# Two phases with buffers of their own for the expert stages of a one-core network

## The chip, the cores and the metric

The kernel runs on one core of a Trainium2 chip. What counts is the device time of one execution, in microseconds. Three executions of the kernel before took 4761.98, 4771.15 and 4781.52 us (median 4771.15).

## The reference

The reference runs two networks one after the other. The first has two layers (`DEPTH` 2); each has a token mixer and then an expert stage, `peer_ffn`, for 256 context tokens and 256 latent tokens of width 1024 (in layer 1 for the latent tokens alone). The second has four layers of attention-like mixers and feed-forward stages. The change touches the two expert stages only:

```python
def peer_ffn(h, wq, subkeys, u, v):
    qr = (h @ wq).astype(jnp.float32).reshape(bsz, t, PEER_HEADS, 2, PEER_HALF)
    scores = jnp.einsum('bthpd,hpkd->bthpk', qr, subkeys.astype(jnp.float32))
    s1, i1 = lax.top_k(scores[..., 0, :], PEER_TOPK)
    s2, i2 = lax.top_k(scores[..., 1, :], PEER_TOPK)
    ...
    top, pos = lax.top_k(cand, PEER_TOPK)
    eidx = jnp.take_along_axis(cidx, pos, axis=-1)
    gate = jax.nn.softmax(top, axis=-1).astype(h.dtype)
    ...
        act = jax.nn.gelu(jnp.einsum('ted,td->te', u[ek], hk), approximate=False)
        return jnp.einsum('te,ted->td', gk * act, v[ek])
```

Each token chooses 16 experts in each of 8 heads out of 16,384 (128 x 128 keys). An expert is a row of `u` and a row of `v`: Gelu of the product with the row of `u`, times the gate, weighs the row of `v`.

## The kernel before

`peer(l)` runs the expert stage of layer l. The first F tokens (128 of 512 in layer 0, 64 of 256 in layer 1) are "fetched": `fetched` gathers the chosen rows of `u` and `v` by indirect DMAs on the POOL queue, 1 MB each, and works on VectorE (two 1024-wide steps a gather). The other ND tokens (384 and 192) are "dense": they are multiplied with all experts, and the gates, zero for experts not chosen, pick them out. The experts come in 128 steps j of 128 experts.

*Routing.* `route` is a generator. `c_q` makes queries and scores, `choose` the top 16 of pairs, `gates` the softmax, and `spread` writes the gates as a dense matrix: for four tokens at a time one-hot rows of i1 (`oa`) and of i2 times the gate (`ob`) on VectorE, four small matmuls, two copies out of PSUM on ScalarE, and then a store to the DRAM tensor G in blocks of 32 tokens.

*First product.* `u_act` multiplies step j of `u` with the dense tokens. In layer 0 the weight and the tokens are split into a high and a low part (`load_w`, `split`: a copy on ScalarE, a subtraction on VectorE), and each of the 8 k-chunks takes three matmuls: high by high, high by low, low by high. In layer 1 (`whole`) the f32 weight is used as it is loaded. `ahead` makes first products during the routing and stores the sums to the DRAM tensor U. How many, and between which routing steps, is set by the costs that `route` yields: as long as PE's sum `tp` is below VectorE's sum `td`, another first product is put in. Layer 0 makes all 128 in the routing. In layer 1, 72 are made there, and the rest in the second phase.

*Second product.* `u_phase(j0)` prepares two steps: loads of the gates G (four steps a load, in runs of 4 x 32 x 4 = 512 bytes) and of the sums U, Gelu, the product with the gate, and the split into high and low, `wt`. For steps that were not made early it calls `u_act`. `v_phase` loads the rows of `v`, splits them and multiplies. In layer 0 the dense tokens are the stationary side: 18 matmuls of 512 columns a step, into six PSUM banks. In layer 1 `v` is: 24 matmuls of 192 columns a step into four banks, two chunks to a bank. The loops are written so that `u_phase` of one pair of steps stands ahead of `v_phase` of the pair before. Beside this, `extra` computes modulation vectors (layer 0) and gathers that are left go on.

*Order and buffers.* All loads and stores here but the gathers are issued by SP in one order. A scheduler orders the instructions by priority (mostly program order) and readiness; each tag has so many buffers, and an instruction that writes a buffer waits for its last reader. Weights of `u` and of `v` share the tag `wraw` (4 buffers in layer 0, 6 in layer 1); `whi` and `wlo` are their high and low parts. `part` opens pools of buffers for the routing (`ROUTE`) and, when these are closed, for the second product (`DENSE`), in the same memory.

Of the kernel before, what the change touches and what calls it, by code (L numbers as in the profile page):

```python
# [10 lines left out]
F32 = mybir.dt.float32  # L11
# [11 lines left out]
P = 128  # L23
# [28 lines left out]
WORKP = (dict(nbig=2048, bufs=4, ga=3, w=(4, 3, 2), mm=2, sm=6, sp=4, uv=4, H=1, acc=1),  # L52
         dict(nbig=2048, bufs=2, ga=3, w=(6, 2, 2), mm=4, sm=4, sp=6, uv=5, H=1, acc=1, xw=1))
ROUTE = dict(bufs=3, rt=1, VI=1, t=3, r=13, alt=1, oa=2, ob=4)
DENSE = dict(bufs=1, gt=2, ad=2, wt=2, o=2)
# [28 lines left out]
class Kern:  # L84
# [634 lines left out]
    def route(self, l, xh, xl, cs, G, F, fetch):  # L719
# [93 lines left out]
        def spread(t):  # L813
            for t0 in range(*own(t), GT):
                st = [self.b8().rearrange("p (j t) -> p j t", t=GT) for _ in range(2)]
                for t4 in range(t0, t0 + GT, 4):
                    pg = self.ps()
                    a = self.t(512, tag="oa").rearrange("p (t n) -> p t n", t=4)
                    nc.vector.tensor_tensor(a, self.iotaf[:, None, :].to_broadcast([P, 4, P]),
                                            i1T[:, t4:t4 + 4, None].to_broadcast([P, 4, P]), op=OP.is_equal)  # L820
                    for i in range(4):
                        t_ = slice(t4 + i, t4 + i + 1)
                        b_ = self.t(P, tag="ob")
                        nc.vector.tensor_scalar(b_, self.iotaf, i2T[:, t_], gT[:, t_], op0=OP.is_equal, op1=OP.mult)
                        nc.tensor.matmul(pg[:, i * P:(i + 1) * P], a[:, i], b_, start=True, stop=True)
# [57 lines left out]
    def peer(self, l, extra=()):  # L883
# [8 lines left out]
        xh, xl = self.big(KD, N, F32R), self.big(KD, N, F32R)  # L892
# [35 lines left out]
        self.part(routing, **ROUTE)  # L928
# [40 lines left out]
        while early < late:  # L969
            ahead()  # L970
            early += 1
# [1020 lines left out]
```

## Time and profile before

| | |
|---|---|
| median of three runs | 4771.15 us |
| profiled execution | 4776.65 us |
| its span, first to last instruction | 4774.9 us |
| mean granted TensorE clock | 0.953 |
| PE busy | 4352.2 us (91%) |
| VectorE (DVE) busy | 3402.8 us (71%) |
| ScalarE (ACT) busy | 2104.5 us (44%) |
| moved by DMA | 948.85 MB, mean 199 GB/s |

A busy PE is a matmul in flight; matmuls overlap, so the duration of one is longer than the distance between two. The clock is given as a share of 2.4 GHz; its other level is 1.2 GHz. The DMA share is the mean busy share of the core's 16 DMA engines. Line numbers (L949) are those of the kernel before, and a tile's name stands for all its buffers. L208 is every activation, L275 and L280 are the subtractions that make a low part, L293 is a matmul of `linear`. L949 and L944 are first products (layer 0 and 1), L1026 and L1019 second products (layer 0 and 1), L825 the small matmuls of `spread`.

### The profile page before, as it was taken

How to read it: one execution, taken by the hardware profiler on the slowest of the kernel's cores; microseconds unless marked ns; L12 is line 12 of the kernel's file. 1: busy time of each engine (PE TensorE's matmuls, PEld its weight loads, DVE VectorE, ACT ScalarE, POOL GpSimd, SP SyncE). 2: the span in 40 equal slices, each digit the busy share in tenths (PEclk: the TensorE clock that was granted, in tenths of full speed). 3: DMA queues.
4: the chain of work that ended last, by engine and by line, in shares of the span. 5: the costliest groups of instructions: out<-in, count | busy, mean ns of one | idle time of the engine just before them, and what ended most of it. 6: DMA issues, size and time to landing. Idle time of an engine off the chain costs nothing. (4 is left out here: it accounts for less than half of the span.)

```text
span 4774.9 us, 72861 instructions
## 1 busy us (share of the span) xinstructions
PE 4352.2 (91%) x27964; PEld 3992.4 (84%) x27964; DVE 3402.8 (71%) x6651; ACT 2104.5 (44%) x4022; POOL 288.9 (6%) x200
## 2 busy tenths in 40 slices
PE   6999798998988999998967799989999999999999
PEld 5887798888876787887856699978998998899799
DVE  9987998899778757978863344477567567566765
ACT  4443344344433445541323233377445454445853
POOL 0000022222011100001220000000000000000000
PEclk8999899999999999999977799999999998999999
DMA  5413388888999874547994468533553553055255
GB/s 191 133 58 104 136 291 323 295 309 329 327 305 337 281 223 130 169 160 282 377 376 146 148 204 266 193 99 103 175 152 108 175 159 100 19 172 165 90 168 172
DMA packets 313101, 948.85 MB, mean 199 GB/s; under 512 B 28832, under 2 KB 130080, under 8 KB 282928
## 3 DMA queue, kind: packets, MB, share of 16 engines
q1 hardware_dynamic: 285104, 742.86, 47.4%
q0 software_dynamic: 27648, 201.34, 11.2%
q8 instruction: 219, 3.59, 0.3%
q14 instruction: 130, 1.06, 0.1%
HBM read 872.70 MB, written 71.04 MB: 198 GB/s over the span
## 5 line engine op out<-in xcount | busy, mean ns | idle before, releaser
L208 ACT ACTIVATE whi<-wraw 128x1024 fp32r<-128x1024 f32 (+1 forms) x924 | 964.3, 1047 | 1337.0 <-PE MM L293 524.3
L293 PE MATMUL MM<-xhl,whi 128*128 128x272 f32 (+1 forms) x4736 | 934.6, 293 | 6.7 <-ACT whi L208 6.1
L275 DVE TENSOR_TENSOR wlo<-wraw,whi 128x1024 fp32r<-128x1024 f32 (+2 forms) x668 | 799.3, 1198 | 161.2 <-PE MM L293 53.1
L293 PE MATMUL MM<-b,whi 128*128 128x272 f32 (+2 forms) x3712 | 855.3, 323 | 59.8 <-ACT b L208 50.0
L293 PEld LDWEIGHTS MM<-xhl,whi 128*128 128x128 f32 x4736 | 751.2, 190 | 27.4 <-issue 10.0
L293 PEld LDWEIGHTS MM<-b,whi 128*128 128x128 f32 x3712 | 623.0, 192 | 115.8 <-ACT b L208 56.5
L293 PE MATMUL MM<-xhl,wlo 128*128 128x272 f32 (+1 forms) x2368 | 689.2, 291 | 2.8 <-DVE wlo L275 2.7
L293 PE MATMUL MM<-b,wlo 128*128 128x272 f32 (+2 forms) x1856 | 597.2, 323 | 5.3 <-DVE wlo L275 4.7
L949 PE MATMUL MM<-b,whi 128*128 128x384 f32 x2048 | 545.4, 347 | 14.2 <-ACT ga L208 13.9
L280 DVE TENSOR_TENSOR wlo<-wraw,whi 128x1024 fp32r<-128x1024 f32 x256 | 311.3, 1222 | 277.4 <-ACT whi L208 206.4
L1019 PE MATMUL SM<-wt,whi 128*128 128x192 f32 x2048 | 399.0, 300 | 103.2 <-ACT whi L208 76.1
L293 PEld LDWEIGHTS MM<-xhl,wlo 128*128 128x128 f32 x2368 | 448.7, 190 | 10.2 <-DVE wlo L275 4.6
L873 POOL DMA_INDIRECT uv<-uv,sp x192 | 287.9, 1499 | 2676.1 <-DVE acc L869 952.0
L1019 PEld LDWEIGHTS SM<-wt,whi 128*128 128x128 f32 x2048 | 352.6, 215 | 106.9 <-ACT whi L208 79.3
L949 PE MATMUL MM<-b,wlo 128*128 128x384 f32 x1024 | 356.0, 349 | 59.0 <-DVE wlo L275 59.0
L949 PEld LDWEIGHTS MM<-b,whi 128*128 128x128 f32 x2048 | 380.2, 195 | 18.6 <-ACT ga L208 17.9
L1026 PE MATMUL SM<-whi,wt 128*128 128x512 f32 x1536 | 380.7, 397 | 13.7 <-ACT wt L208 8.0
L293 PEld LDWEIGHTS MM<-b,wlo 128*128 128x128 f32 x1856 | 355.7, 192 | 31.2 <-DVE wlo L275 10.0
L944 PE MATMUL MM<-xw,wraw 128*128 128x192 f32 x2048 | 359.1, 332 | 10.5 <-ACT ga L208 9.9
L1026 PEld LDWEIGHTS SM<-whi,wt 128*128 128x128 f32 x1536 | 293.7, 192 | 82.1 <-ACT wt L208 10.7
L944 PEld LDWEIGHTS MM<-xw,wraw 128*128 128x128 f32 x2048 | 339.7, 194 | 12.5 <-ACT ga L208 11.6
L1019 PE MATMUL SM<-wt,wlo 128*128 128x192 f32 x1024 | 305.0, 298 | 15.2 <-DVE wlo L280 15.2
(488 smaller groups left out, 6096.8 us busy)
## 6 DMA issues: line engine op xcount, KB each, us to landing
wraw<-uT SPq DMA_DIRECT2D x256, 512.0 KB
wraw<-uv SPq DMA_DIRECT2D x256, 512.0 KB
wraw<-w_gate_up SPq DMA_DIRECT2D x176, 512.0 KB
g<-b SPq DMA_DIRECT2D x36, 1024.0 KB
wraw<-w_in SPq DMA_DIRECT2D x64, 512.0 KB
wraw<-fox_w_in SPq DMA_DIRECT2D x64, 512.0 KB
wraw<-w_down SPq DMA_DIRECT2D x64, 512.0 KB
wmod<-wmodT SPq DMA_DIRECT2D x56, 512.0 KB
```

The source lines that it names most:

```text
L208: r = nc.scalar.activation(out, in_, func, **kw)
L275: nc.vector.tensor_sub(lo[:, :n], raw[:, :n], hi[:, :n].bitcast(F32))
L280: self.nc.vector.tensor_sub(lo, src, hi.bitcast(F32))
L293: nc.tensor.matmul(ps, w_, x_[k, slice(a, b)], start=(i == 0 and q == 0), stop=(i == kc - 1 and q == 2))
L873: nc.gpsimd.indirect_dma_start(z, None, self.A[f"uv{l}"], bass.IndirectOffsetOnAxis(ap=ids[:, js], axis=0))
L944: nc.tensor.matmul(ps, raw[:, k * P:(k + 1) * P], xw[:, k], start=k == 0, stop=k == KD - 1)
L949: nc.tensor.matmul(ps, w_[:, k * P:(k + 1) * P], x_[k, dc], start=(k == 0 and q == 0), stop=(k == KD - 1 and q == 2))
L1019: nc.tensor.matmul(half(c), w_[:, c * P:(c + 1) * P], x_[:, jj], start=j == 0 and q == 0 and c % 2 == 0, stop=j == P - 1 and q == 2, skip_ ...
L1026: nc.tensor.matmul(res[c][h], w_[:, jj, c * P:(c + 1) * P], v[:, h * 512:(h + 1) * 512], start=(j == 0 and q == 0 and i == 0), stop=(j == ...
```

## The change

All 128 first products of both layers are made in the routing phase: as before between the routing's steps, but at most 124, and the rest behind it, with gathers in between (one for 10 us of estimated time). The Gelu is applied as the sums leave PSUM, and U holds its result. All products with the high part come ahead of those with the low part. `spread` makes both sets of one-hot rows by one VectorE instruction each, and the gate is multiplied in by four ScalarE copies with a scale.

The second product loads gates for eight steps (runs of 1 KB), one group ahead; U for four steps, two groups ahead; and `v` into buffers of its own (`vr`, 5 and 6), 4 and 5 steps ahead. In layer 1 the high part of `v` is multiplied with high and low weights side by side (384 columns), the low part with the high weights (192 columns), a bank for each of the eight chunks, and the two halves are added at the end. `xh` and `xl`, the split tokens, move into the routing's pool. In layer 0 `whi` has two buffers in place of three; in layer 1 `MM` has two banks in place of four, `SM` six in place of four, and `uv` four buffers in place of five.

The functions that are dropped (`u_phase`, `v_phase`) are left out of the diff; they stand above.

```diff
-WORKP = (dict(nbig=2048, bufs=4, ga=3, w=(4, 3, 2), mm=2, sm=6, sp=4, uv=4, H=1, acc=1),
-         dict(nbig=2048, bufs=2, ga=3, w=(6, 2, 2), mm=4, sm=4, sp=6, uv=5, H=1, acc=1, xw=1))
-ROUTE = dict(bufs=3, rt=1, VI=1, t=3, r=13, alt=1, oa=2, ob=4)
-DENSE = dict(bufs=1, gt=2, ad=2, wt=2, o=2)
+WORKP = (dict(nbig=2048, bufs=0, ga=3, w=(4, 2, 2), mm=2, sm=6, sp=4, uv=4, H=1, acc=1),
+         dict(nbig=2048, bufs=0, ga=3, w=(6, 2, 2), mm=2, sm=6, sp=6, uv=4, H=1, acc=1))
+ROUTE = (dict(bufs=7, rt=1, VI=1, t=3, r=13, alt=1, oa=3, ob=2), dict(bufs=5, rt=1, VI=1, t=4, r=16, alt=2, oa=4, ob=2, xw=1))
+DENSE = (dict(bufs=0, gt=2, ad=3, wt=2, vr=5, o=2), dict(bufs=0, gt=2, ad=3, wt=2, vr=6, o=2))
+
+LAST = 4
...
-                    a = self.t(512, tag="oa").rearrange("p (t n) -> p t n", t=4)
-                    nc.vector.tensor_tensor(a, self.iotaf[:, None, :].to_broadcast([P, 4, P]),
-                                            i1T[:, t4:t4 + 4, None].to_broadcast([P, 4, P]), op=OP.is_equal)
+                    ohs = []
+                    for z in (i1T, i2T):
+                        o = self.t(512, tag="oa")
+                        nc.vector.tensor_tensor(o.rearrange("p (t n) -> p t n", t=4),
+                                                self.iotaf[:, None, :].to_broadcast([P, 4, P]),
+                                                z[:, t4:t4 + 4, None].to_broadcast([P, 4, P]), op=OP.is_equal)
+                        ohs.append(o)
+                    b_ = self.t(512, tag="ob")
                     for i in range(4):
-                        t_ = slice(t4 + i, t4 + i + 1)
-                        b_ = self.t(P, tag="ob")
-                        nc.vector.tensor_scalar(b_, self.iotaf, i2T[:, t_], gT[:, t_], op0=OP.is_equal, op1=OP.mult)
-                        nc.tensor.matmul(pg[:, i * P:(i + 1) * P], a[:, i], b_, start=True, stop=True)
+                        ts = slice(i * P, (i + 1) * P)
+                        self.actv(b_[:, ts], ohs[1][:, ts], AF.Copy, scale=gT[:, t4 + i:t4 + i + 1])
+                        nc.tensor.matmul(pg[:, ts], ohs[0][:, ts], b_[:, ts], start=True, stop=True)
...
-        xh, xl = self.big(KD, N, F32R), self.big(KD, N, F32R)
...
-        self.part(routing, **ROUTE)
+        self.part(routing, **ROUTE[l])
+        xh, xl = self.big(KD, N, F32R), self.big(KD, N, F32R)
...
-        def u_act(j, func):
+
+        early, tp, td = 0, 0.0, HEAD[l]
+
+        def ahead():
+            nonlocal early
+            j = early
+            early += 1
...
-                for k in range(KD):
-                    nc.tensor.matmul(ps, raw[:, k * P:(k + 1) * P], xw[:, k], start=k == 0, stop=k == KD - 1)
+                terms = [(raw[:, k * P:(k + 1) * P], xw[:, k]) for k in range(KD)]
...
-            for k in range(0 if whole else KD):
-                for q, (w_, x_) in enumerate(((hi, xh), (hi, xl), (lo, xh))):
-                    nc.tensor.matmul(ps, w_[:, k * P:(k + 1) * P], x_[k, dc],
-                                     start=(k == 0 and q == 0), stop=(k == KD - 1 and q == 2))
+                terms = [(hi[:, k * P:(k + 1) * P], z[k, dc]) for k in range(KD) for z in (xh, xl)]
+                terms += [(lo[:, k * P:(k + 1) * P], xh[k, dc]) for k in range(KD)]
+            for i, (w_, x_) in enumerate(terms):
+                nc.tensor.matmul(ps, w_, x_, start=i == 0, stop=i == len(terms) - 1)
             a = self.t(max(ND, D // 2), tag="ga")[:, :ND]
-            self.actv(a, ps, func)
-            return a
...
-        early, tp, td = 0, 0.0, HEAD[l]
-
-        def ahead():
-            nc.sync.dma_start(U[:, early], u_act(early, AF.Copy))
+            self.actv(a, ps, AF.Gelu)
+            nc.sync.dma_start(U[:, j], a)
+
         done = 0
         for pe, dve in self.route(l, xh, xl, cs, G, F, fetch):
             n = fetch_for(dve, EVERY[l])
             done += n
             tp, td = tp + pe, td + dve + n * 2.55
-            while tp < td and early < P:
+            while tp < td and early < P - LAST:
                 ahead()
-                early, tp, td = early + 1, tp + ND * CU[l], td + (0.0 if whole else 1.1)
-        late = min(P, -(-early // 4) * 4 + 4)
-        while early < late:
+                tp, td = tp + ND * CU[l], td + (0.0 if whole else 1.1)
+        while early < P:
             ahead()
-            early += 1
-
+            done += fetch_for(ND * CU[l], 10.0)
         routing.close()
-        self.part(dense, **DENSE)
+        self.part(dense, **DENSE[l])
         left = F - done
...
-        res = [[self.ps() for _ in range(2)] for _ in range(nd)] if nd else [self.ps() for _ in range(4)]
-        half = lambda c: res[c // 2][:, c % 2 * 256:c % 2 * 256 + ND]
-        held = {}
-
...
+        res = [[self.ps() for _ in range(2)] for _ in range(nd)] if nd else [self.ps("SM" if c < 6 else "MM")
+                                                                             for c in range(KD)]
+        J, JU, JG = 2, 4, 8
+        gts, ads, raws = {}, {}, {}
+        b3 = lambda z: z.rearrange("p (b t) -> p b t", t=GT)
+
+        def load_g(n):
+            if n < P // JG:
+                gt = self.t(JG * ND, tag="gt")
+                gts[n] = gt.rearrange("p (b j t) -> p j b t", j=JG, t=GT)
                 nc.sync.dma_start(gt.rearrange("p (b j) -> p b j", b=nb),
-                                  G[:, :nb, j0:j0 + 4].rearrange("p b j t -> p b (j t)"))
-                if j0 < early:
...
+                                  G[:, :nb, n * JG:(n + 1) * JG].rearrange("p b j t -> p b (j t)"))
+
+        def load_u(n):
+            if n < P // JU:
+                ads[n] = self.t(JU * ND, tag="ad").rearrange("p (j t) -> p j t", j=JU)
+                nc.sync.dma_start(ads[n], U[:, n * JU:(n + 1) * JU])
+
+        def load_v(j):
+            if j < P:
+                raws[j] = self.t(D, tag="vr")
+                nc.sync.dma_start(raws[j], A[f"uv{l}"].rearrange("(p j) d -> p j d", j=P)[:, j, D:])
+
+        def gated(j0):
+
+            if j0 % JG == 0:
+                load_g(j0 // JG + 1)
+            if j0 % JU == 0:
+                load_u(j0 // JU + 2)
+            wt = self.t(J * 2 * ND, F32R, "wt").rearrange("p (j s t) -> p j s t", j=J, s=2)
+            a = ads[j0 // JU][:, j0 % JU:j0 % JU + J]
+            for jj in range(J):
+                nc.vector.tensor_mul(b3(a[:, jj]), b3(a[:, jj]), gts[j0 // JG][:, j0 % JG + jj])
+            self.split(a, wt[:, :, 0], wt[:, :, 1])
+            return wt
+
+        def products(j0, wt):
             for jj in range(J):
                 j = j0 + jj
-                raw = self.w.tile([P, 1024], F32, name="wraw", bufs=self.wb[0])
-                nc.sync.dma_start(raw, A[f"uv{l}"].rearrange("(p j) d -> p j d", j=P)[:, j, D:])
+                load_v(j + VR)
                 vh, vl = (self.w.tile([P, 1024], F32R, name=n, bufs=b) for n, b in zip(("whi", "wlo"), self.wb[1:]))
-                self.split(raw, vh, vl)
-                if not nd:
+                self.split(raws.pop(j), vh, vl)
...
+                if nd:
...
+                                    nc.tensor.matmul(res[c][h], wt[:, jj, s_, c * P:(c + 1) * P],
...
+                else:
+                    both = wt[:, jj].rearrange("p s t -> p (s t)")
                     for c in range(KD):
-                        for q, (w_, x_) in enumerate(((vh, wh), (vh, wl), (vl, wh))):
-                            nc.tensor.matmul(half(c), w_[:, c * P:(c + 1) * P], x_[:, jj],
-                                             start=j == 0 and q == 0 and c % 2 == 0, stop=j == P - 1 and q == 2,
-                                             skip_group_check=True)
-                for q, ws, v in ((0, (wh, wl), vh), (1, (wh,), vl)) if nd else ():
...
+                        nc.tensor.matmul(res[c][:, :2 * ND], vh[:, c * P:(c + 1) * P], both, start=first, stop=end,
+                                         skip_group_check=True)
+                    for c in range(KD):
+                        nc.tensor.matmul(res[c][:, :ND], vl[:, c * P:(c + 1) * P], wt[:, jj, 0], start=False, stop=end,
+                                         skip_group_check=True)
+
+        VR = DENSE[l]["vr"] - 1
+        load_g(0)
+        load_u(0)
+        load_u(1)
+        for j in range(VR):
+            load_v(j)
...
-            w = u_phase(j0)
+            w = gated(j0)
             if prev is not None:
-                v_phase(*prev)
+                products(*prev)
                 next(extra, None)
                 fetch_for(left, P // J - 1)
-            prev = (j0, *w)
-        v_phase(*prev)
+            prev = (j0, w)
+        products(*prev)
...
+        for c in range(0 if nd else KD):
+            xs = x[c, slice(cs[0] + F, cs[1])]
+            for s_ in range(2):
+                nc.vector.scalar_tensor_tensor(xs, res[c][:, s_ * ND:(s_ + 1) * ND], M(0, 5)[:, c:c + 1], xs,
+                                               op0=OP.mult, op1=OP.add)
...
-        for c in range(0 if nd else KD):
-            xs = x[c, slice(cs[0] + F, cs[1])]
-            nc.vector.scalar_tensor_tensor(xs, half(c), M(0, 5)[:, c:c + 1], xs, op0=OP.mult, op1=OP.add)
```

## Rows read from the trace of the kernel before

**Rows 1.** Stage table: stretch, us, busy per engine (instructions), TensorE clock, DMA share, GB/s.

```profile
core 0: us, PE busy (x) PEld busy (x) DVE busy (x) ACT busy (x) POOL busy (x), PEclk, DMA share, GB/s
600.00:1240.00 640.00, 585.19 (x3461) 569.92 (x3462) 556.30 (x1015) 260.63 (x599) 139.98 (x85) 0.97 0.86 309
1240.00:1600.00 360.00, 317.73 (x1302) 249.64 (x1301) 290.35 (x394) 145.95 (x220) 54.98 (x34) 0.96 0.93 326
...
1700.00:1833.00 133.00, 133.00 (x588) 110.14 (x587) 63.11 (x71) 55.24 (x60) 0.00 (x0) 1.00 0.58 184
...
2160.00:2436.00 276.00, 233.15 (x1445) 226.01 (x1444) 230.17 (x507) 71.47 (x253) 51.31 (x43) 0.93 0.91 346
2436.00:2806.00 370.00, 251.56 (x1698) 243.62 (x1696) 152.93 (x218) 108.69 (x171) 21.30 (x14) 0.76 0.57 193
2806.00:3107.00 301.00, 301.00 (x2290) 301.00 (x2289) 139.45 (x210) 106.61 (x202) 6.56 (x7) 1.00 0.71 231
```

**Rows 2.** The chain of waits, layer 1's second product: start, us, what.

```profile
2806.72 5.22 PE MM L944 x32
2811.94 5.34 PE SM L1019 x48
```

**Rows 3.** Timeline of SP's queue, one period: start, us, issues.

```profile
2606.70 0.53 SPq L987 DMA_DIRECT2D gt<-g  x1
2608.12 10.37 SPq L1013 DMA_DIRECT2D wraw<-uv  x4
2618.63 1.03 SPq L991 DMA_DIRECT2D ad<-u  x1
...
2625.76 0.53 SPq L987 DMA_DIRECT2D gt<-g  x1
```

**Rows 4.** Waits in 2500 to 2806: us in total, times, longest.

```profile
ACT ad L208 <- DMA ad<-u: 109.5, 15, 13.2
```

**Rows 5.** Groups of instructions, 600 to 1240: busy us, mean ns, idle before.

```profile
L949 PE MATMUL MM<-b,wlo 128*128 128x384 f32 x896 | 310.7, 347 | 45.2 <-DVE wlo L275 45.2
...
L824 DVE TENSOR_SCALAR ob<-iotaf,rt 128x128 f32<-128x128 f32 x384 | 110.5, 351 | 7.4 <-PE SM L825 4.4 <-PE MM L949 3.0
...
L819 DVE TENSOR_TENSOR oa<-iotaf,rt 128x512 f32<-128x512 f32 x96 | 65.4, 681 | 0.0
...
L208 ACT ACTIVATE rt<-SM 128x128 f32<-128x128 f32 x9 | 1.8, 280 | 0.0
```

**Rows 6.** Groups of VectorE's instructions, 2500 to 2806.

```profile
L280 DVE TENSOR_TENSOR wlo<-wraw,whi 128x1024 fp32r<-128x1024 f32 x65 | 78.3, 1223 | 101.4 <-ACT whi L208 101.4
L280 DVE TENSOR_TENSOR wt<-ad,wt 128x384 fp32r<-128x384 f32 x32 | 17.6, 551 | 0.0
```

**Rows 7.** Timeline of PE: layer 0's first products; the border in layer 1.

```profile
743.08 0.51 PE L949 MATMUL MM<-b,whi 128*128 128x384 f32 x2
743.42 0.33 PE L949 MATMUL MM<-b,wlo 128*128 128x384 f32 x1
743.60 0.51 PE L949 MATMUL MM<-b,whi 128*128 128x384 f32 x2
...
745.16 1.05 PE L825 MATMUL SM<-ob,oa 128*128 128x128 f32 x8
...
2466.23 1.17 PE L1019 MATMUL SM<-wt,whi 128*128 128x192 f32 x4 [26.71 <-ACT wt L208]
```

**Rows 8.** Stage table again, two stretches of layer 1.

```profile
2330.00:2436.00 106.00, 94.08 (x611) 89.65 (x610) 91.67 (x201) 32.37 (x119) 21.69 (x19) 0.98 1.00 393
...
2600.00:2640.00 40.00, 28.87 (x199) 28.04 (x198) 13.82 (x20) 11.55 (x16) 0.00 (x0) 0.79 0.50 148
```

**Rows 9.** DMA traffic and issues, 2500 to 2806.

```profile
DMA packets 23570, 47.76 MB, mean 156 GB/s; under 512 B 1552, under 2 KB 13072, under 8 KB 23394
...
wraw<-uv SPq DMA_DIRECT2D x60, 512.0 KB
```

**Rows 10.** DMA issues of the whole run: first-product stores of layer 1.

```profile
u<-ga SPq DMA_DIRECT2D x72, 96.0 KB
```

More of the change, by code (lines that the diff above doesn't have):

```diff
@@ L973, in peer @@
         routing.close()
-        self.part(dense, **DENSE)
+        self.part(dense, **DENSE[l])
         left = F - done
-        J = 2
         nd = ND // P if ND % P == 0 else 0
-        res = [[self.ps() for _ in range(2)] for _ in range(nd)] if nd else [self.ps() for _ in range(4)]
-        half = lambda c: res[c // 2][:, c % 2 * 256:c % 2 * 256 + ND]
-        held = {}
-        def u_phase(j0):
-            if j0 % 4 == 0:
-                gt = self.t(4 * ND, tag="gt")
-                held["g"] = gt.rearrange("p (b j t) -> p j b t", j=4, t=GT)
-                nc.sync.dma_start(gt.rearrange("p (b j) -> p b j", b=nb),
-                                  G[:, :nb, j0:j0 + 4].rearrange("p b j t -> p b (j t)"))
-                if j0 < early:
-                    held["u"] = self.t(4 * ND, tag="ad").rearrange("p (j t) -> p j t", j=4)
-                    nc.sync.dma_start(held["u"], U[:, j0:j0 + 4])
-            wt = self.t(4 * ND, F32R, "wt").rearrange("p (j t) -> p j t", j=4)
-            wh, wl = wt[:, 0:2], wt[:, 2:4]
-            b3 = lambda z: z.rearrange("p (b t) -> p b t", t=GT)
-            if j0 < early:
-                a = held["u"][:, j0 % 4:j0 % 4 + 2]
-                self.actv(a, a, AF.Gelu)
-                for jj in range(2):
-                    nc.vector.tensor_mul(b3(a[:, jj]), b3(a[:, jj]), held["g"][:, j0 % 4 + jj])
-                self.split(a, wh, wl)
-            else:
-                for jj in range(J):
-                    a = u_act(j0 + jj, AF.Gelu)
-                    nc.vector.tensor_mul(b3(a), b3(a), held["g"][:, j0 % 4 + jj])
-                    self.split(a, wh[:, jj], wl[:, jj])
-            return wh, wl
@@ L1022, in v_phase @@
-                for q, ws, v in ((0, (wh, wl), vh), (1, (wh,), vl)) if nd else ():
-                    for c in range(nd):
-                        for h in range(2):
-                            for i, w_ in enumerate(ws):
-                                nc.tensor.matmul(res[c][h], w_[:, jj, c * P:(c + 1) * P], v[:, h * 512:(h + 1) * 512],
-                                                 start=(j == 0 and q == 0 and i == 0), stop=(j == P - 1 and q == 1))
+                self.split(raws.pop(j), vh, vl)
@@ new lines, in products @@
+                first, end = j == 0, j == P - 1
+                if nd:
+                    for q, ss, v in ((0, (0, 1), vh), (1, (0,), vl)):
+                        for c in range(nd):
+                            for h in range(2):
+                                for s_ in ss:
+                                    nc.tensor.matmul(res[c][h], wt[:, jj, s_, c * P:(c + 1) * P],
+                                                     v[:, h * 512:(h + 1) * 512], start=first and q == 0 and s_ == 0,
+                                                     stop=end and q == 1)
+                else:
+                    both = wt[:, jj].rearrange("p s t -> p (s t)")
+                    for c in range(KD):
+                        nc.tensor.matmul(res[c][:, :2 * ND], vh[:, c * P:(c + 1) * P], both, start=first, stop=end,
[3 more added lines that the diff above has]
+                                         skip_group_check=True)
@@ L1053, in add @@
                                                    op0=OP.mult, op1=OP.add)
-        if F < P:
-            fold = self.t(F, tag="sp")
-            nc.vector.tensor_copy(fold, self.ident[:, :F])
-            for r in range(F, P, F):
-                nc.vector.tensor_add(fold, fold, self.ident[:, r:r + F])
-        add(0, F, acc, fold if F < P else self.ident)
+        for c in range(0 if nd else KD):
[3 more added lines that the diff above has]
+                                               op0=OP.mult, op1=OP.add)
+        if F:
+            fold = self.ident
+            if F < P:
+                fold = self.t(F, tag="sp")
+                nc.vector.tensor_copy(fold, self.ident[:, :F])
+                for r in range(F, P, F):
+                    nc.vector.tensor_add(fold, fold, self.ident[:, r:r + F])
+            add(0, F, acc, fold)
         for c in range(nd):
```

1 line of the change is left out of this document (removed).

## Prediction

> **What bounds the kernel now.** I read the stage table first: the span cut at the borders of the two expert stages [rows 1]. Layer 0 routes until 1240 and runs its second product until 1833; layer 1 routes until 2436 and runs its second product until 3107. The reader should read down the PE and DMA columns. In 600 to 1240 PE is 91% busy and DMA 0.86; in four others PE is full or DMA above 0.9. The exception is 2436 to 2806: PE 252 of 370 us, clock 0.76, DVE 153, DMA 0.57. Nothing is full there, so something waits for something that isn't asked for in time.
>
> The chain of waits gives the rest of layer 1: from 2806 on it is PE alone, alternating 5.22 us of 32 first-product matmuls with 5.34 us of 48 second-product matmuls, one pair of steps in 10.56 us [rows 2]. A step is one j, 128 experts. So 2806 to 3107 is bound by PE and 2436 to 2806 is not.
>
> What is late there is read from SP's queue [rows 3]. In a period of some 19 us SP issues one gate load, four V loads that take 10.37 us to issue because each needs a free weight buffer, and only then the load of the first-product sums (`ad<-u`). ACT, which has to apply Gelu to these sums first, stands idle for them 109.5 us in 306 [rows 4]. The U load has no depth: it is queued behind V loads that wait for the buffers which this very step frees. 60 V loads go in 306 us, 5.1 us a step [rows 9], where PE needs 2.67.
>
> **The change part by part.** The sum is made against the profiled execution, 4776.65 us (span 4774.9 and 1.75 around it), which lies 5.5 above the median of the three timed runs, 4771.15.
>
> *1. Layer 1, first products all in phase one.* 72 of 128 were made early [rows 10]. The other 56 now follow the routing with nothing beside them but gathers. Each is 16 matmuls, 5.22/2 = 2.61 us [rows 2]: 56 x 2.61 = 146 us. Their U rows and stores are 0.62 MB in 2.61 us, 238 GB/s, and 15 gathers in this time (one per 10 us by the new call) bring about 105 more; 343 lies under the 393 GB/s that the end of the routing reached [rows 8]. So I take PE's price. This is no new work: those 56 lay between the second products before and leave from there.
>
> *2. Layer 1, second product in two wider passes.* 8 matmuls of 384 columns with the high half of V, 8 of 192 with the low half, in place of 24 of 192. 192 columns cost 5.34/48 = 0.111 us [rows 2]. 384 columns: three in 0.52 us, 0.173 each [rows 7]. So 8 x 0.173 + 8 x 0.111 = 2.28 us a step, 292 for 128, against 342. The DVE has 1.22 for V's low half, 0.35 for the gate product (the other half of its work on `ad`) and 0.55/2 for the low half of the weight: 1.85 us [rows 6], below PE. (The 0.35 is my estimate, between the 0.55 us of 384 columns and half of it.)
>
> *3. Layer 1, loads ahead.* V gets five or six buffers of its own, U is asked for two groups ahead, gates one group of eight. The stall of [rows 3, 4] goes, because neither U nor gates wait behind a V of the same step. What is late next is the traffic itself: 0.524 MB V, 0.098 U, 0.098 gates, 0.72 MB a step. The DMA engines took 0.50 of 40 us for 148 GB/s, so 296 GB/s while busy [rows 8]; the same division gives 317, 325 and 339 for the last three second-product stretches of [rows 1]. At 320 a step takes 2.25 us. Some 6 to 10 of the 21 gathers that were issued after 2436 [rows 1] remain, 1.05 MB each, 0.2 us a step: 2.45. In layer 0's second product engines at 0.93 already left PE waiting [rows 1], so I take a little more, 2.55 us a step, 326 us. Ends: PE's 2.28 (gates in 1 KB runs go faster) and 2.9 (296 GB/s and all 21 gathers).
>
> A rule of the Trainium skill speaks against the change. The busy share and the bytes of V-heavy traffic give 296 GB/s [rows 8], and V is 31.5 of 47.76 MB there [rows 9]. The Trainium skill, "DMA: Bandwidth & Descriptors", section "Latency and other measured facts", says that copies whose rows lie a large power of two apart in HBM slow down, 207 GB/s at a pitch of 512 KiB and 164 at 2 MiB. V's partitions lie 1 MiB apart (128 rows of 8 KB), so an estimate by that page is 185 GB/s for V. The trace disagrees: with two thirds of the bytes at 185 and the rest at 393 the mix could not pass 226 GB/s.
>
> *4. The border between the phases.* The dense buffers now lie where the routing's `xh`, `xl` and `b8` tiles were, so the first gate and U loads can only start when the last first product is done. Gates 0.79 MB, two U groups 0.79, V 0.52 at 345 GB/s (the middle of [rows 8]) are 6 us, 2 for latency, some 4 for splits: 12 us in layer 1; gates and U are twice that in layer 0, 15 us. The row to compare is the border of before, 26.7 us of idle PE in layer 1 [rows 7], none in layer 0. Ends 5 and 27 each.
>
> Layer 1 from 2436: 671 us become 146 + 12 + 326 = 484, so -187.
>
> *5. Layer 0, second product.* Its matmuls don't change: 588 in 133 us, 0.226 each [rows 1], 18 a step, 4.07 us, 521 us in all, against 593. PE idled or ran slow mostly before 1600, when DMA was at 0.93 [rows 1]. Gates in 1 KB runs and V five ahead smooth that, but the bytes stay. I take 521 + 15 (border) + 20 of remaining waits = 556, so -37. Ends: +10 (waits stay, border 15 is added and a little is won) and -60. The Gelu leaves ACT here, which isn't on the path.
>
> *6. Routing, gates spread on ACT.* For four tokens one DVE compare of 0.681 and four of 0.351 (2.09 us) become two of 0.681 (1.36) and four ACT copies of 128 columns, 0.28 each by the nearest row [rows 5]: DVE -0.72, ACT +1.12 a group. 96 groups in layer 0: DVE -69 of 556, ACT +108 on 261 in 640 us [rows 1]. Layer 1, 48 groups: DVE -35, ACT +54 on 71. PE lost 640 - 567 = 73 us in layer 0's stretch (2684 matmuls at 0.173 and 768 at 0.131 [rows 7], the rest is waiting or half clock), of which 45.2 is waiting for the low half of U [rows 5]. The new order (16 products with the high half, then 8 with the low) gives that half 2.8 us more, and DVE is less full. I take -40 of the 73. Ends: -65 and, if PE waits for ACT in place of DVE, +50. The high half has two buffers in place of three; it is now free after two thirds of a product, which covers it. Layer 1: PE idles 43 of 276 us, but DMA is busy for 0.91 x 276 = 251 [rows 1], so no more than 25 is to be had: -15, ends -25 and +25. Gelu in place of Copy on the way out of PSUM costs the same kind of ACT pass; I put it at nothing, covered by ACT's idle 40%.
>
> *7. Small.* Eight more vector steps on the result in layer 1, under the 0.55 us of 384 columns [rows 6], some 0.4 each: +3.
>
> Sum: -187 - 37 - 40 - 15 + 3 = -276, so 4776.65 - 276 = 4500 us.
>
> **Rivals.**
> (a) *PE is the only bound.* Then layer 1 is 146 + 12 + 292 = 450 (-221), layer 0's second product 536 (-57), routing -60 and -25: -360, 4417 us. For it: DMA's full-share rate of 393 [rows 8]. Against: the 0.93 beside idle PE in 1240 to 1600 [rows 1].
> (b) *V's rows are slow when they come alone.* Before, V shared the engines with contiguous U rows or came in bursts of four. Four V loads took SP 10.37 us to issue [rows 3]; if that is the pace at which they can run, V takes 2.6 us, with 0.49 for gates and U at 393 GB/s and 0.2 for gathers 3.3 a step, 422 in place of 326: 4596. Against it: that pace was set by buffers, and the busy share gives 296 GB/s [rows 8]. By the rule of the page named above, 185 GB/s, it would be 3.5 a step and 4625.
> (c) *ACT takes DVE's place in the routing.* ACT works in order; its copies stand behind casts that wait for a weight buffer, PE waits for the copies. 144 groups x 1.12 = 161 us are added; with half of it exposed and the 55 of gain lost, 4500 + 80 + 55 = 4635. For it: PE already waits for these one-hot rows. Against: ACT is 41% busy in layer 0, 26% in layer 1 [rows 1].
> (d) *Slower: the wait stays and spreads to all steps.* SP issues in order. If the new gate or U loads sit behind V loads that wait for buffers, as in [rows 3], all 128 steps of layer 1 go at 5.1 us: 653 in place of 326, 4827. It decides above 2.55 + 276/128 = 4.7 us a step. Against: U is asked for eight steps ahead, and a V load waits only for a split one step back.
>
> **How the numbers follow.** Forecast 4500 with 0.56 (its own range 4440 to 4570), (a) 0.17, (b) 0.11, (c) 0.10, (d) 0.05, and 0.01 for no effect. The range 4405 to 4630 takes in (a), (b) and most of the ends above (they don't all fall on one side); it leaves out (d), the worse half of (c) and what is better than (a). Half a per cent, 24 us, is what a measurement here can tell from no change. Faster 0.92, within it 0.03, slower 0.05.
>
> **What would show it.** Layer 1: a stretch of PE alone on first products after the routing (146 us), then 128 steps at 2.55 us with DMA above 0.9; below 2.4 is (a), 3.3 is (b), 5 is (d). PE's clock there near 1.00. ACT's wait for `ad` gone from the list of waits. Border gaps near 15 and 12 us. Layer 0's second product near 541 us without its border. In the routing DVE 69 us lower and PE's wait for the low half below 20 us; PE waiting for `ob` by ACT would be (c). The forecast is wrong if layer 1 after its routing takes more than 560 us.

## The result and the profile after

The changed kernel takes 4651.44 us (median of 4 runs, 4640.08 to 4668.60) against 4766.56 (4761.58 to 4781.52) for the kernel before: ratio 0.9756, 95% interval 0.9718 to 0.9795, so 2.4% faster. The forecast was 4500 us with a range of 4405 to 4630: the direction was right, the size was not, and the median lies above the range. The profiled execution of the changed kernel took 4640.08 us with a span of 4638.2, 136.7 below the span before. In what follows stages are read from the profiled executions.

The stage table of the changed kernel, cut at its own borders, answers to [rows 1]: layer 0 routes to 1202.5 and runs its second product from 1221 to 1789.5; layer 1's first products end at 2542.3, its second product runs from 2553 to 2965.

```profile
600.00:1205.00 605.00, 564.77 (x3415) 556.51 (x3413) 520.30 (x731) 373.66 (x981) 129.31 (x87) 0.98 0.90 327
1205.00:1560.00 355.00, 313.00 (x1309) 255.15 (x1310) 298.01 (x409) 124.17 (x190) 60.01 (x34) 0.93 0.93 347
1560.00:1790.00 230.00, 226.70 (x1001) 187.17 (x1000) 109.87 (x126) 80.84 (x84) 0.00 (x0) 1.00 0.57 187
...
2160.00:2378.00 218.00, 187.03 (x1133) 182.28 (x1134) 167.62 (x240) 116.88 (x418) 53.36 (x39) 0.91 0.98 373
2378.00:2545.00 167.00, 159.10 (x968) 156.74 (x966) 39.49 (x48) 26.49 (x93) 14.09 (x15) 1.00 0.94 331
...
2553.00:2965.00 412.00, 338.61 (x2048) 328.15 (x2048) 231.35 (x334) 168.07 (x210) 5.98 (x4) 0.89 0.70 235
```

The last row is the one to read. Layer 1's second product has 292 us of matmuls and takes 412, with DMA at 0.70, VectorE (third busy column) at 231 us and the clock at 0.89. Again nothing is full. Layer 0's second product missed its forecast too: 568.5 us from its first to its last matmul, forecast 541. Stage by stage, change forecast and measured:

| stage | forecast | changed kernel | changed kernel with the order rule (e1) |
|---|---|---|---|
| layer 0, routing | -40 | -37 | -36 |
| layer 0, second product with its border | -37 | -6 | -41 |
| layer 1, whole expert stage | -199 | -96 | -180 |
| everything else | 0 | +2 | -1 |
| sum | -276 | -137 | -258 |

What PE waited for in layer 1's second product (us in total, times, longest), and, over about the same stretch (2560 to 2960), what VectorE and SP's queue waited for:

```profile
PE SM L1040 <- DVE wlo L282: 73.0, 31, 9.9
```

```profile
DVE ad L1015 <- DMA ad<-u: 103.2, 25, 7.4
```

```profile
SPq L1004 <- DVE wlo L282: 243.4, 119, 10.9
```

PE waits for the low half of V (L282), VectorE for a U load, at its gate product (L1015), and SP's V loads (L1004) for VectorE. The wait for U has gone from ScalarE, which had the Gelu, to VectorE: 109.5 us for 60 steps in [rows 4, 9], 103.2 for some 125 steps now, and 23.5 more at the same gate product that the profile puts down to a V load, which the gate product doesn't read.

The waits are not the whole loss. Of the 120 us above the matmuls' 292, PE is idle for 73. The other 47 go with a lower clock: PE is busy 338.6 us with the matmuls that take 292 at the full one. PE's timeline at one of the waits, then six wide matmuls soon after it and six more 7 us later; below them the stage row of the stretch behind the wait:

```profile
2698.99 1.59 PE L1040 MATMUL SM<-wt,wlo 128*128 128x192 f32 x6 [2.90 <-DVE wlo L282]
...
2700.80 2.18 PE L1037 MATMUL SM<-wt,whi 128*128 128x384 f32 x6
...
2707.61 1.24 PE L1037 MATMUL SM<-wt,whi 128*128 128x384 f32 x6
```

```profile
2700.60:2705.00 4.40, 4.40 (x18) 4.40 (x18) 1.69 (x2) 1.58 (x2) 0.00 (x0) 0.50 0.81 261
```

The granted clock of that stretch is 0.50, the 1.2 GHz level, and 0.96 from 2705.0 to 2711.7.

VectorE's timeline over one and a half periods shows how the wait comes about:

```profile
2690.33 1.23 DVE L282 TENSOR_TENSOR wlo<-vr,whi 128x1024 fp32r<-128x1024 f32 x1 [0.52 <-ACT whi L210]
2696.64 1.16 DVE L1015 TENSOR_TENSOR ad<-ad,gt 128x192 f32<-128x192 f32 x4 [5.08 <-DMA ad<-u]
2697.72 1.22 DVE L282 TENSOR_TENSOR wlo<-vr,whi 128x1024 fp32r<-128x1024 f32 x1
2698.85 0.55 DVE L282 TENSOR_TENSOR wt<-ad,wt 128x384 fp32r<-128x384 f32 x1
2699.32 1.22 DVE L282 TENSOR_TENSOR wlo<-vr,whi 128x1024 fp32r<-128x1024 f32 x1
2701.10 1.23 DVE L282 TENSOR_TENSOR wlo<-vr,whi 128x1024 fp32r<-128x1024 f32 x1 [0.56 <-issue]
2702.24 0.55 DVE L282 TENSOR_TENSOR wt<-ad,wt 128x384 fp32r<-128x384 f32 x1
2705.37 1.23 DVE L282 TENSOR_TENSOR wlo<-vr,whi 128x1024 fp32r<-128x1024 f32 x1 [2.57 <-ACT whi L210]
2709.35 1.16 DVE L1015 TENSOR_TENSOR ad<-ad,gt 128x192 f32<-128x192 f32 x4 [2.76 <-DMA ad<-u]
```

and SP's queue in the same time:

```profile
2689.83 0.34 SPq L999 DMA_DIRECT2D ad<-u  x1
2691.59 11.10 SPq L1004 DMA_DIRECT2D vr<-uv  x4
2702.82 0.34 SPq L999 DMA_DIRECT2D ad<-u  x1
2706.62 0.33 SPq L1004 DMA_DIRECT2D vr<-uv  x1
```

One period is four steps, 12.7 us here, 3.1 to 3.2 a step. The gate products come four at a time, a whole group, where the program asks for two ahead of each pair of steps. The U load issued at 2702.82 is the 14th, and the gate products at 2709.35, which wait for it, are those of the 14th group, steps 52 to 55 (52 gate products were done before). PE is at the start of step 43 then, and 43 V splits are done. In the program this gate product stands behind the V split of step 49, here it follows that of step 42. So the scheduler, which takes instructions by readiness in its own model, moved the gate product some seven steps up, to just behind the point where a U buffer comes free (the weight split at 2702.24, which reads the last of group 10). There it meets a load that needs 6.5 us to land. The V splits that PE needs now are queued behind it on VectorE. The ring closes: U load lands, gate products, V splits, weight split, buffer free, next U load. SP's order runs beside it: the four V loads from 2691.59 on, which wait for V splits, end 0.1 us before the U buffer comes free. The Trainium skill, "TensorE: Matmul & The Clock Gate", section "Architectural detail: the array is 16× 32×32, not 1× 128×128", says that VectorE's queue is strictly first in, first out. The trace agrees: in the lines above no V split passes a waiting gate product.

### The profile page after: what moved, and what is told of

Same layout as the page of the kernel before. It is cut to its first block, busy times and chain, and to the rows that moved or that the text cites. A ratio compares the mean times of both kernels' runs of the same rounds, so it can differ in the third digit from the quotient of the medians.

```text
span 4638.2 us, 71261 instructions
## 1 busy us (share of the span) xinstructions
PE 4273.5 (92%) x26940; PEld 3930.3 (85%) x26940; DVE 3330.0 (72%) x6199; ACT 2220.0 (48%) x4474; POOL 282.1 (6%) x200
## 5 line engine op out<-in xcount | busy, mean ns | idle before, releaser
L210 ACT ACTIVATE whi<-wraw 128x1024 fp32r<-128x1024 f32 (+2 forms) x668 | 695.5, 1043 | 758.4 <-PE MM L295 547.2
L295 PEld LDWEIGHTS MM<-b,whi 128*128 128x128 f32 x3712 | 623.0, 192 | 114.3 <-ACT b L210 55.8
L210 ACT ACTIVATE whi<-vr 128x1024 fp32r<-128x1024 f32 x256 | 270.7, 1058 | 411.1 <-PE SM L1031 183.9
L961 PE MATMUL MM<-b,whi 128*128 128x384 f32 x2048 | 399.2, 345 | 15.0 <-ACT ga L210 15.0
L1031 PE MATMUL SM<-whi,wt 128*128 128x512 f32 x1536 | 377.3, 395 | 18.5 <-ACT whi L210 18.5
L282 DVE TENSOR_TENSOR wlo<-vr,whi 128x1024 fp32r<-128x1024 f32 x256 | 310.4, 1219 | 103.3 <-ACT whi L210 81.2
L961 PEld LDWEIGHTS MM<-b,whi 128*128 128x128 f32 x2048 | 365.3, 194 | 17.5 <-ACT ga L210 16.8
L880 DVE SCALAR_TENSOR_TENSOR ga<-uv,H 128x1024 bf16<-128x1024 f32 x192 | 233.6, 1218 | 178.6 <-DMA u<-ga 138.7
L875 DVE SCALAR_TENSOR_TENSOR acc<-uv,sp,acc 128x1024 f32<-128x1024 f32 x190 | 242.9, 1278 | 39.2 <-ACT sp L210 38.3
L1015 DVE TENSOR_TENSOR ad<-ad,gt 128x384 f32<-128x384 f32 (+1 forms) x256 | 103.2, 452 | 219.6 <-DMA ad<-u 196.1
```

The lines of the kernel that those rows point to most:

```text
L210: r = nc.scalar.activation(out, in_, func, **kw)
L282: self.nc.vector.tensor_sub(lo, src, hi.bitcast(F32))
L295: nc.tensor.matmul(ps, w_, x_[k, slice(a, b)], start=(i == 0 and q == 0), stop=(i == kc - 1 and q == 2))
L875: nc.vector.scalar_tensor_tensor(acc, v, w[:, j:j + 1], acc, op0=OP.mult, op1=OP.add)
L880: nc.vector.scalar_tensor_tensor(self.t(D, BF, tag="ga"), z[:, :D], 1.0, H, op0=OP.mult, op1=OP.mult, accum_out=act[:, js])
L961: nc.tensor.matmul(ps, w_, x_, start=i == 0, stop=i == len(terms) - 1)
```

## The experiments

Times are medians with the ratio to the kernel before as it ran beside them. "Second product" is from its first to its last matmul.

**e1, the order rule.** One dependency in the scheduler, without a wait on the chip, keeps the gate product behind the V split that stands ahead of it in the program.

```diff
-                nc.vector.tensor_mul(b3(a[:, jj]), b3(a[:, jj]), gts[j0 // JG][:, j0 % JG + jj])
+                m = nc.vector.tensor_mul(b3(a[:, jj]), b3(a[:, jj]), gts[j0 // JG][:, j0 % JG + jj])
+                if last:
+                    self.after(m.ins, last[-1].ins)
...
-                self.split(raws.pop(j), vh, vl)
+                last.append(self.split(raws.pop(j), vh, vl))
```

> The changed kernel with one more rule for the order on VectorE: the gate product of a pair of steps stays behind the split of the V rows that the program has ahead of it (in the changed kernel it was moved up about seven steps and stood waiting for its U load, with the V splits queued behind it). Theory 1, the moved gate product and the U load wait for each other in a ring through SP's queue: layer 1's second product falls from 412 us (3.2 a step) to 300 to 330 (2.35 to 2.55), layer 0's from 568 to about 545, in all 95 to 135 us below the changed kernel. Theory 2, V rows come slowly when they come alone (3.2 us a step is their pace): no change beyond 10 us in layer 1. Theory 3, three U buffers are too few for a landing time of 6.8 us: no change beyond 20 us, since their number is the same.

4519.78 us, ratio 0.9469 (0.9454 to 0.9485), 132 us below the changed kernel. Layer 1's second product takes 312 us, layer 0's 530 (569 before the rule). The stage table for layer 1's second product, VectorE's timeline and PE's waits in it:

```profile
2536.00:2848.00 312.00, 302.03 (x2046) 300.03 (x2047) 234.63 (x336) 165.39 (x210) 6.68 (x4) 0.97 0.92 311
```

```profile
2694.31 0.62 DVE L1015 TENSOR_TENSOR ad<-ad,gt 128x192 f32<-128x192 f32 x2
2694.99 1.23 DVE L282 TENSOR_TENSOR wlo<-vr,whi 128x1024 fp32r<-128x1024 f32 x1
2697.28 1.23 DVE L282 TENSOR_TENSOR wlo<-vr,whi 128x1024 fp32r<-128x1024 f32 x1 [1.07 <-ACT whi L210]
2698.43 0.55 DVE L282 TENSOR_TENSOR wt<-ad,wt 128x384 fp32r<-128x384 f32 x1
2698.89 0.62 DVE L1015 TENSOR_TENSOR ad<-ad,gt 128x192 f32<-128x192 f32 x2
```

```profile
PE SM L1042 <- DVE wlo L282: 9.5, 5, 4.5
```

The same instructions with the same buffers, two gate products at a time, 4.58 us for two steps: 2.29 a step, PE's price of 2.28. The 20 us that the stage takes above 292 lie in its first 40, where the last four gathers run (POOL's column); behind these PE is busy throughout at the full clock:

```profile
2536.00:2576.00 40.00, 30.03 (x148) 28.03 (x149) 31.64 (x44) 15.85 (x27) 6.68 (x4) 0.80 0.96 372
2576.00:2650.00 74.00, 74.00 (x518) 74.00 (x517) 56.38 (x83) 40.52 (x48) 0.00 (x0) 1.00 0.96 316
```

The V loads still wait long for VectorE on SP (190.7 us from 2560 to 2850), and that harms nobody now. Theory 1 holds, theories 2 and 3 fall.

**e2, five U buffers in layer 1** (`ad=5`, U asked for four groups ahead).

> The changed kernel with five U buffers in layer 1 in place of three, and U asked for four groups ahead in place of two. Theory 1: the gate product is moved up further by as much as the buffers allow and waits as before, so layer 1's second product stays at 395 to 420 us. Theory 3, too few buffers: it falls to about 330 us. Theory 2: 412 us as it was.

4657.29 us, ratio 0.9766 (0.9747 to 0.9785); layer 1's second product takes 420 us. VectorE in that kernel still stands 4.69 us before a whole group of gate products:

```profile
2705.42 1.17 DVE L1015 TENSOR_TENSOR ad<-ad,gt 128x192 f32<-128x192 f32 x4 [4.69 <-DMA vr<-uv]
```

Two more buffers bought nothing, as theory 1 has it: the scheduler has moved the gate product further up. These are steps 56 to 59 (56 gate products were done before), and only 39 V splits are done; the program has 54 ahead of them. So it stands some 15 steps up, in place of seven. The wait is again put down to a V load, which the gate product doesn't read; over the stage the profile puts 96.4 us of it down to U loads and 23.4 to V loads.

**e3, V from contiguous rows** (`raws[j]` is loaded from `uT`).

> The changed kernel where the second product reads rows of u, 512 KB in one piece, in place of the rows of v that lie 1 MiB apart from partition to partition; same bytes, same instructions, other data. Theory 2, the pitch of V's rows sets the pace: layer 1's second product falls from 412 to 330 us or less, layer 0's by 10 to 30. Theory 1: the ring is set by the landing time of U and by the engines, so layer 1 stays within 390 to 412 us. Theory 3: as theory 1.

4621.22 us, ratio 0.9685 (0.9669 to 0.9701); layer 1's second product 381 us, layer 0's 562. 31 us less in layer 1: below theory 1's band, far from theory 2's 330. The median U load lands in 6.0 us there against 6.8, and its landing is in the ring. That fits, but the question whether V's pitch costs DMA time by itself needed a kernel without the ring.

**e7, the same with the order rule.**

> The kernel with the order rule, and the second product reads 512 KB pieces of u in place of v's rows (1 MiB apart from partition to partition); other data, same bytes. With the order rule DMA is 0.92 busy and layer 1's second product takes 312 us, 20 above PE's 292. If the pitch of v's rows costs DMA time: 292 to 300 us, DMA share 0.8 to 0.85 at a higher rate. If it doesn't: 307 to 315 us.

4507.21 us, ratio 0.9447 (0.9420 to 0.9475); layer 1's second product 310 us against 312.

```profile
2540.00:2840.00 300.00, 290.92 (x2003) 289.14 (x2002) 229.10 (x327) 163.19 (x206) 4.29 (x3) 0.99 0.90 311
```

The DMA share is 0.90 at 311 GB/s against 0.92 at the same rate. So the pitch costs at most some 2 us in layer 1's second product (the medians are 13 us apart over the whole kernel, with ratio intervals that overlap). The time alone could not show more, since PE is the limit of e1 from 2576 on; the share at an equal rate can. The rule of the Trainium skill, "DMA: Bandwidth & Descriptors", section "Latency and other measured facts", which puts copies with such a pitch near 185 GB/s by my estimate, does not hold for these loads: with V at nearly three quarters of the traffic (0.524 of 0.72 MB a step), e1 moved 311 GB/s. (Its row was measured with copies between two HBM tensors, 16 KiB a partition; V is loaded into SBUF, 4 KB a partition.)

**e8, the kernel before with the order rule alone.** Gelu and gate product stay behind the V split ahead of them; nothing else of the change.

```diff
-                self.actv(a, a, AF.Gelu)
+                g = self.actv(a, a, AF.Gelu)
+                if last:
+                    self.after(g.ins, last[-1][0].ins)
...
+                    if last:
+                        self.after(m.ins, last[-1][1].ins)
```

> The kernel before with the order rule alone: Gelu and gate product of a pair of steps stay behind the split of the V rows that the program has ahead of them. Theory 1, the hoisted work in front of the V splits makes the ring: the early part of layer 1's second product (first of its matmuls at 2466, 72 steps in 340 us, 4.7 a step) falls to 200 to 280 us, the whole kernel by 50 to 130 us. Rival, U loads that stand behind V loads in SP's one queue are enough to make the ring: 320 to 345 us as it was, the whole within 25 us.

4621.01 us, ratio 0.9679 (0.9647 to 0.9711), which is below the changed kernel's median (the intervals of the two ratios do not overlap). In the early part of layer 1's second product two steps now take 5.36 us (2.68 a step, PE's price for 24 narrow products), from 9.5 before. One of its periods on VectorE, and the start of the next:

```profile
2503.76 0.55 DVE L280 TENSOR_TENSOR wt<-ad,wt 128x384 fp32r<-128x384 f32 x1
2504.22 0.62 DVE L1001 TENSOR_TENSOR ad<-ad,gt 128x192 f32<-128x192 f32 x2
2505.30 1.22 DVE L280 TENSOR_TENSOR wlo<-wraw,whi 128x1024 fp32r<-128x1024 f32 x1 [0.45 <-ACT whi L208]
2507.98 1.23 DVE L280 TENSOR_TENSOR wlo<-wraw,whi 128x1024 fp32r<-128x1024 f32 x1 [1.46 <-ACT whi L208]
2509.12 0.55 DVE L280 TENSOR_TENSOR wt<-ad,wt 128x384 fp32r<-128x384 f32 x1
2509.59 0.62 DVE L1001 TENSOR_TENSOR ad<-ad,gt 128x192 f32<-128x192 f32 x2
```

So the stall of layer 1 in the kernel before was the same kind of ring, and neither buffers of V's own nor a deeper U load was needed to open it. On SP a U load still follows four V loads in e8, with the gate load now between the second and the third. The kernel before had shown it: its gate products too came four at once, behind ScalarE's Gelu.

```profile
2605.51 1.16 DVE L999 TENSOR_TENSOR ad<-ad,gt 128x192 f32<-128x192 f32 x4 [6.67 <-ACT ad L208]
```

Layer 0 is another matter. Its second product takes 576 us in e8 in place of 593, and PE waits for the low half of V as it did, 33.4 us and 31.6 before. The changed kernel has 29.3 there, and with the order rule 2.0:

```profile
PE SM L1031 <- DVE wlo L282: 29.3, 9, 8.9
```

```profile
PE SM L1033 <- DVE wlo L282: 2.0, 2, 1.0
```

So in layer 0 neither the rule alone nor the change alone removes this wait, and the two together do.

**e4 and e6, the routing's two edits undone one at a time.** e4 has the old spread (with its numbers of buffers for the one-hot rows), e6 the old order of layer 0's first products (high, high, low for each chunk).

```diff
-                terms = [(hi[:, k * P:(k + 1) * P], z[k, dc]) for k in range(KD) for z in (xh, xl)]
-                terms += [(lo[:, k * P:(k + 1) * P], xh[k, dc]) for k in range(KD)]
+                terms = [(w_[:, k * P:(k + 1) * P], z[k, dc]) for k in range(KD)
+                         for w_, z in ((hi, xh), (hi, xl), (lo, xh))]
```

> The changed kernel with the gates spread as before (four VectorE instructions for the rows with the gate, none on ScalarE). If the lighter VectorE gave the 37 us that layer 0's routing won, they go back: routing of layer 0 30 to 40 us longer. If the order of the products (all high parts first) gave them, it is within 10 us of the changed kernel. Layer 1's routing, which became 5 us longer: 10 to 20 us shorter if PE's waits for ScalarE's copies cost it, unchanged or longer if DMA is its limit.

> The changed kernel with layer 0's first products in the old order (high, high, low for each chunk). The old spread gave back only 10 of the 37 us that layer 0's routing won. If the order of the products gave the rest: the last first product of layer 0 goes from 1202 to 1222 to 1235, and PE waits 25 to 45 us for the low half, as before. If it is something else (three buffers instead of two for the one-hot rows, the tokens' place), it stays within 8 us of 1202.

e4: 4686.65 us (0.9823, 0.9801 to 0.9845); layer 0's first products end 10 us later, layer 1's phase one is 519 us in place of 498. e6: 4679.66 us (0.9818, 0.9787 to 0.9848); layer 0's first products end 24 us later. PE's wait for the low half of U in layer 0 from 600 on, of the changed kernel and then of e6:

```profile
PE MM L961 <- DVE wlo L277: 7.7, 6, 2.9
```

```profile
PE MM L961 <- DVE wlo L277: 19.6, 9, 7.0
```

10 + 24 of the 37 us of layer 0 are so accounted for, two thirds of it by the order of the products. e6's wait lay below what I expected (25 to 45); that the lighter VectorE remains there may be why, and isn't shown. In layer 1 the old spread made phase one 21 us longer. That is the way of my second reading, but its ground, DMA as the limit, fell: the share in the routing is 0.89 with e4 and 0.98 in the changed kernel. What grew is PE's wait for ScalarE at the first product's sums (`ga`), 39.4 us with e4 and 21.0 without. So the new spread saves some 20 us there, and something else takes as much. What it is stays open; the other kernels with the same routing code have phase one at 498 to 514 us, so part is scatter.

**e5, buffers of their own for the sums** (with the order rule, layer 1: `ua=4`, `ga=2`; so far the sums shared three `ga` buffers with the gathers' scratch).

> The kernel with the order rule, and in layer 1 four buffers of their own for the first-product sums on their way to U, which until now shared three buffers with the gathers' scratch tile (VectorE waited some 120 us for U stores there, and PE some 28 us for ScalarE). Theory 1a, the shared buffers cost PE its waits in phase one of layer 1: the stretch from the first to the last first product of layer 1 (514 us with the order rule, 498 in the changed kernel) falls to 475 to 490. Rival: DMA at 0.95 to 0.98 busy is the limit there, and it stays at 495 to 515.

4497.57 us, ratio 0.9435 (0.9406 to 0.9464), 22 below e1, though the intervals of the ratios overlap a little. The gain isn't where I looked: phase one takes 502 us (514 in e1, 498 in the changed kernel), but the second product 297 us in place of 312. The gathers are done before it begins:

```profile
2525.00:2822.00 297.00, 295.83 (x2047) 295.49 (x2048) 219.28 (x316) 161.80 (x197) 0.00 (x0) 0.99 0.90 306
```

POOL's column has no gather left there; with e1 there were 4. At 0.99 of the clock and 296 of 297 us busy PE is the limit.

**e9, narrow products again,** on e5: 24 matmuls of 192 columns a step.

> The kernel with the order rule and own sum buffers, with layer 1's second product in three passes of 192 columns again (24 matmuls a step), all else kept. The forecast's price for a step was 2.67 us narrow and 2.28 wide. If PE is the limit of layer 1's second product: it goes from 297 us to 340 to 350. If DMA is (0.92 busy): 297 to 315.

4549.00 us, ratio 0.9540 (0.9518 to 0.9563); the second product of layer 1 takes 347 us, PE busy throughout. The wide passes are worth 50 us, as the prices 2.67 and 2.28 say (128 x 0.39).

```profile
2540.00:2840.00 300.00, 300.00 (x2679) 300.00 (x2678) 191.39 (x276) 140.90 (x167) 0.00 (x0) 1.00 0.84 277
```

**e10, gates in 512-byte runs again,** on e5, the same depth in steps.

> The kernel with the order rule and own sum buffers, with gates loaded for four steps at a time in runs of 512 bytes again, two groups ahead into four buffers (the same memory and the same depth in steps). If short runs cost DMA time that matters: layer 1's second product 305 to 330 us in place of 297, layer 0's 540 to 560 in place of 532, DMA share up. If not: both within 6 us.

4505.72 us, ratio 0.9456 (0.9437 to 0.9476). Layer 1's second product stays at 297 us, with a DMA share of 0.93 at 305 GB/s where e5 has 0.90 at 306:

```profile
2532.00:2829.40 297.40, 296.79 (x2048) 296.28 (x2048) 219.57 (x317) 161.91 (x197) 0.00 (x0) 0.99 0.93 305
```

Layer 0's is 539 in place of 532. The short runs cost some 3 to 4% of DMA time, and as DMA isn't quite the limit only a few microseconds, if any: the intervals of e5 and e10 overlap.

**e11, U stores on ScalarE's queue,** on e5 (`nc.scalar.dma_start(U[:, j], a)`).

> The kernel with the order rule and own sum buffers, with the stores of first products to U issued by ScalarE's queue in place of SP's. There PE waited 27 us for U rows in layer 1's phase one; if these loads wait on SP behind stores that wait for their Gelu, phase one (first to last first product of layer 1, 502 us) falls to 475 to 490 and the whole by 10 to 30 us. If DMA's rate is the limit: within 8 us. ScalarE's issue time could cost a little in layer 0's routing.

4492.28 us, ratio 0.9431 (0.9409 to 0.9454): the lowest of all, though not apart from e5. Phase one of layer 1 is 503 us as with e5, PE's wait for U rows 16.4 us in place of 27. Moving the stores out of SP's order isn't what phase one lacks.

## Why the prediction was wrong, step by step

The step that failed is number 3, "loads ahead": "The stall of [rows 3, 4] goes, because neither U nor gates wait behind a V of the same step." It didn't go. I priced 2.55 us a step, and it was 3.22 (412/128), 86 us more in all than the 326 forecast. Of the 120 us above PE's price 73 are waiting, and the rest goes with a clock of 0.89 where I had forecast near 1.00. I had named the place of the stall rightly and its cause wrongly: I read SP's order, U behind four V loads, as the ring, while the order on VectorE and ScalarE closed it. e8 removes the ring from layer 1 of the kernel before, with U loads that still follow V loads on SP and the same buffers; e2 adds U depth to the changed kernel and removes nothing. Whether U loads ahead of the V loads on SP would also have opened the ring, no run shows.

Rival (d) said that the wait stays and put its price at 5.1 us a step; the wait did stay, by another path and at a smaller price. The Gelu is no longer in the ring. The four V issues still stand ahead of a U load (11.10 us from 2691.59 on), but they end as the U buffer comes free. How much of the smaller price each of these makes up isn't shown. The time of a step, 3.22 us, came near the 3.3 that I had given as the sign of rival (b). That is chance: V's rows were not the cause (e3, e7). Nor was (c), ScalarE in the routing (e4).

The order on VectorE spoiled step 5 too. Layer 0's second product was to win 37 us and won 6; with the order rule it wins 41 (e1). My ground for the waits there, DMA at 0.93, was not what held it: with the rule the share is 0.97 and PE's wait for the low half of V falls from 29.3 to 2.0 us.

With the ring gone the prices of the other steps show. A step of layer 1 takes 2.44 us in e1 and 2.32 in e5 (297/128), between PE's 2.28 and the 2.55 that I took; what lies above PE's price in e1 lies in the first 40 us, beside the last gathers. Step 2 was right (e9). Step 4's borders were 18.5 and 10.7 us of idle PE (forecast 15 and 12). Step 6 was right in layer 0 (-37 for -40), with both of the causes that it names.

In layer 1, steps 1 and 6 together were 22 us off: phase one was to grow by 146 - 15 = 131 us and grew by 153 (345 to 498). Of the first products 61 and not 56 stand behind the last matmul of `spread` (976 matmuls in 165 us, 2.7 us each). In the kernel before the loop that rounds up to a group of four had made four to seven of the 72; these moved from the routing to the stretch behind it, and the 153 count both. DMA was busy 0.98 of that routing, as the upper bound of step 6 had warned, but e5 takes 502 us for phase one with DMA at 0.86 and 0.88 in its two parts, so this cause isn't shown and stays open.

Two sums of the prediction are a little off and change nothing: the upper end of step 3 comes to 3.0 us a step and not 2.9, and the new order gives the low half 2.4 us more and not 2.8, since two matmuls stood ahead of it before.

Against e1, which is the change without the ring, the sum of 4500 is 20 us off.

## What to carry to other kernels

When an engine stands idle for a load while nothing is full, look at what is queued behind the waiting instruction on that engine, and at how far ahead of its use the waiting instruction stands: a scheduler that fills gaps by a model moves work for later steps in front of work for this one, and more buffers let it move further (seven steps with three U buffers, 15 with five). Four gate products in a row where the program writes two were the sign. The cure was an order rule of a few lines; try that before a new set of buffers, and price a stall as removed only when every engine's order in it has been followed.

## What the runs showed of the hardware

V loads whose partitions lie 1 MiB apart moved at the same total rate as contiguous ones, 311 GB/s at 0.92 and 0.90 DMA share (e1 and e7, with the loads of U and gates beside them). Gate loads in runs of 512 bytes in place of 1 KB raised the DMA share from 0.90 to 0.93 at about the same rate (e5 and e10). A U load of 384 KB took 6.8 us to land (median) with the DMA engines 0.70 busy and 8.3 us at 0.92 (changed kernel and e1), so a depth in steps has to be reckoned with such landing times, not with the 1.3 us that its bytes would take at the 311 GB/s of e1. And where PE waited its clock was lower too: layer 1's second product has a granted clock of 0.89 with 73 us of waits (changed kernel), and 1.00 from 2576 on in e1, where PE doesn't wait.
